# The feed-forward half as seven products of quarter matrices (Strassen's scheme), over three pairs of 366-column segments

## The chip, the cores and the metric

The kernel runs on one core of one Trainium2 chip. The metric is the device time of one execution in microseconds (us). Five engines of the core matter: PE (TensorE, the matmuls; its weight loads are listed as PEld), DVE (VectorE), ACT (ScalarE), POOL (GpSimd) and SP (SyncE, which here only issues DMAs). Each runs its own instructions in the order of the program; between engines, semaphores make an instruction wait for another's result. PE writes its sums to eight PSUM banks; everything else lives in SBUF, or in DRAM behind DMAs.

## The reference

One layer of a streaming encoder, on 2192 tokens (128 sample tokens of 8 streams, 16 meta tokens, 2048 prompt tokens) of 1024 channels. The first half is two mixers (an RWKV-7 and an mLSTM) with projections in and out, which the change doesn't touch. The second half is the feed-forward:

```
x  = x + concat(yA, yB) @ w_out
x  = x + (SiLU(dwconv3_causal(h2 @ W_act)) * (h2 @ W_gate)) @ w_down,  h2 = RMSNorm(x)
then one final RMSNorm.
```

W_act and W_gate are 1024 x 2816 each, w_down is 2816 x 1024, all float32. The convolution has three causal taps per channel.

## The kernel before, in words

Channels lie on the partitions (8 tiles of 128), tokens in the columns. The tokens are cut into six segments, one of 272 and five of 384 columns.

All large products are made of float32r matmuls: each operand is split into a high part (a cast on ACT) and a low part (the difference, on DVE), and each 128x128 weight tile against a segment takes three matmuls: high x high, high x low, low x high (`gemm`, L309 to L320).

The feed-forward (from L1131) goes over three groups of two segments. In each group 22 steps f make one tile of W_act and one of W_gate (`load_w`, L364: a DMA on SP's queue, the cast at L374, the difference through `tt` at L259), 24 matmuls of 8 input tiles each per segment; then the convolution and SiLU of the first (L1219 to L1239: PSUM is copied out to `ub`, one tap is a tensor_scalar at L1234, two are scalar_tensor_tensor at L1236, tanh on ACT at L1238, L1239), the product with the second at L1240 and the split of the result, gh on ACT (L1243) and gw on DVE and POOL in turns. After 4 or 5 such steps (CHUNKS) the down products of these f run: for each of 8 output tiles d and each segment 12 or 15 matmuls, and one DVE addition into the residual x (L1259). At the end of a group comes the final norm and the store (`rstd`, L1266, L1268). Weights are loaded and split again in each of the three groups.

The normed input h2 of the first two segments is made inside the first half (`ffn_acts`, L1055), in pools that both halves share, so the first feed-forward matmuls of the program's order stand among the last of the mixers. The output projection of the last segment (`last_out`, L1183) runs inside the feed-forward, in the first group's last chunk.

What sets the order: the kernel is written stage by stage, and the framework's scheduler orders the instructions of each engine from a simulated timeline and priorities (the table KN moves stages in it, `ranked`). PSUM's eight banks are rings by tag: gm 2, a 1, m 1, iv 2, ch 2.

Of the kernel before, what the change touches and what calls it, by code (L numbers as in the profile page):

```python
# [39 lines left out]

def staggered(segs, lag):
    """(tile, segment) pairs: each tile for all segments, a later segment lag tiles behind the one before."""
    return [(t - i * lag, g) for t in range(KD + lag * (len(segs) - 1)) for i, g in enumerate(segs) if 0 <= t - i * lag < KD]

# [12 lines left out]
def consts():  # L57
# [3 lines left out]
    c["ident"] = np.eye(128)  # L61
    c["id64"] = (s[:, None] == t[None]).astype(float)
# [15 lines left out]
    c["one"] = np.ones((128, 1))  # L78
# [14 lines left out]
# Places in the scheduler's order, engines, PSUM rings and buffer counts of the stages.  # L93
# [118 lines left out]
def trunk_kernel(ctx: ExitStack, tc: tile.TileContext, A):  # L212
# [50 lines left out]
    wp = ctx.enter_context(tc.tile_pool(name="wp", bufs=1))  # L263
    big = ctx.enter_context(tc.tile_pool(name="big", bufs=2))

    cst = cp.tile([128, CONST.shape[1]], F32, name="cst")
# [3 lines left out]
    def C(n, rows=128):  # L270
        o, w = COFF[n]
        return cst[:rows, o:o + w]
# [8 lines left out]
    ident, id64, blk, one = C("ident"), C("id64"), C("blk"), C("one")  # L281
# [55 lines left out]
    def token_sums(pr, acc, n):  # L337
        """Sums over the channels, tokens on the partitions."""
# [9 lines left out]
    def split_acts(name, half, n, src=None, scale=None, raws=None):  # L348
        """float32r parts of an activation tile: src is loaded, scale(raw, k, j) fills or scales tile k in raw[:, j]."""
# [14 lines left out]
    def load_w(src, cache=None):  # L364
        """float32r parts of a weight tile; parts that come again are kept in DRAM."""
# [21 lines left out]
    def pt(tag, shape=(128, 512)):  # L387
        """A bank, in the shape asked for."""
# [6 lines left out]
    with ExitStack() as p1:  # L395
        pool = lambda n, b, **k: p1.enter_context(tc.tile_pool(name=n, bufs=b, **k))
        kp = pool("kp", 1)
# [10 lines left out]
        nc.sync.dma_start(cst, A["cst"])  # L408
# [42 lines left out]
        def build_h0():  # L451
            """The first segment's activations: squares are summed over the channels by ones on the tensor engine."""
# [50 lines left out]
        def shifted(w, h, s, ct, out):  # L503
            """Projected columns of tile ct, each mixed with the token before it."""
# [115 lines left out]
        def rwkv(u, s, ws, h, lo1, lo2):  # L620
# [157 lines left out]
            def chain():  # L778
# [4 lines left out]
                def sb(t, h):  # L783
                    """S' and the rank-one updates' left factors of head h."""
# [101 lines left out]
        def conv4(w, h, s, j, out):  # L886
            """Projected columns, causal conv of four taps and SiLU; j is the channel tile of q|k."""
# [142 lines left out]
        def out_proj(s, ds):  # L1030
            """Residual plus the projected mixers' output, kept in DRAM."""
# [23 lines left out]
        def ffn_acts(s):  # L1055
            """The normed input of the second half, for the segments that come first there."""
            n = SEGS[s][1]
            rb = pt("gm")
            bcast(rb, rsd[:, s], n)
            return split_acts("h2", s, n, xd[s], lambda r, k: V.scalar_tensor_tensor(  # L1060
                r, r, PR("nf", k), rb[:, :n], op0=ALU.mult, op1=ALU.mult))

# [3 lines left out]
        H = {}  # L1066
# [12 lines left out]
        for s, u, hd in slots:  # L1079
# [36 lines left out]
            if s == len(SEGS) - 1 and u == 3:  # L1116
                with rank("h20"):
                    H[0] = ffn_acts(0)
            if u is None:
                with rank("h21"):  # L1120
                    H[1] = ffn_acts(1)
# [9 lines left out]
    with ExitStack() as p2:  # L1131
        pool = lambda n, b, **k: p2.enter_context(tc.tile_pool(name=n, bufs=b, **k))
        kp = pool("kp2", 1)
        accp = pool("acc", 4)
        gp = pool("gp", 1)
        ep = pool("ep2", 2)
        sp = pool("sp2", 2)
        rings = {x: itertools.cycle([t for t in y for _ in range(banks[t])]) for x, y in (("up", ("gm", "a")), ("dn", ("iv", "m")), ("rb", ("ch",)))}

        def pt2(use):  # L1140
            return pt(next(rings[use]), (128, NW))

        fst = kp.tile([128, NFF, 8, 2], F32, name="fst")
        nc.scalar.dma_start(fst, A["st_ffn"])
        h_f = kp.tile([128, NFF, 2], F32, name="h_f")
        so_ffn = kp.tile([128, NFF, 9, 2], F32, name="so_ffn")

        @ranked("sqs")
        def square_sum(acc, src, k, n):
            if k == 0:  # L1150
                S.activation(acc[:, :n], src, AF.Square)
                return
            q = ep.tile([128, NW], F32, name="nsq", tag="nsq")
            S.activation(q[:, :n], src, AF.Square)
            (V if k == KD - 1 else G).tensor_tensor(acc[:, :n], acc[:, :n], q[:, :n], op=ALU.add)

        @ranked("rstd")
        def rstd(acc, n):
            ss = token_sums(pt2("rb"), acc, n)
# [10 lines left out]
        def kparts(h, n):  # L1170
            return [(h[0][:, k, :n], h[1][:, k, :n]) for k in range(KD)]
# [181 lines left out]
```

## Time and profile before

| | |
|---|---|
| time, median of 3 runs | 3524.24 us (3522.81 to 3527.25) |
| profiled execution, span of its instructions | 3507.6 us |
| PE busy | 3411.7 us (97%) |
| DVE busy | 2146.4 us (61%) |
| ACT busy | 1152.2 us (33%) |
| POOL busy | 941.0 us (27%) |
| feed-forward, last mixer matmul to last matmul | 1877 to 3489 us |

The span is the time from the first to the last instruction of the one execution that the profiler took; the profile lists no other time of that execution. The median of the runs is 16.6 us above the span. Busy shares are means over two halves with different limits, so they are read by stretch below. A name such as ps_gm is a PSUM bank by its tag, w a split weight tile, h2hi and h2lo the split input.

### The profile page before, as it was taken

Reading aid. Unit: us, or ns where it says so; the run is one execution under the profiler, and the core shown is the slowest. Engines: PE = TensorE matmul, PEld = TensorE weight load, DVE = VectorE, ACT = ScalarE, POOL = GpSimd, SP = SyncE. Lnnn points to the kernel's source line nnn. Section 1 sums busy time; section 2 is a strip of 40 time slices with the busy share of each in tenths; the row PEclk is TensorE's granted clock in tenths of the full one; section 3 lists DMA queues with packets and bytes.
Section 4 is the critical chain, followed back from the end, with each engine's and each line's share of the span. In section 5 each row is a group of like instructions: output and inputs, shape, how many; then the busy total and the mean of one; then the engine's idle time right before and its main releaser. Section 6 shows DMA issues by size and latency. Waiting matters only on the chain.

```text
span 3507.6 us, 63114 instructions
## 1 busy us (share of the span) xinstructions
PE 3411.7 (97%) x24228; PEld 3123.6 (89%) x24228; DVE 2146.4 (61%) x5529; ACT 1152.2 (33%) x2826; POOL 941.0 (27%) x2294
## 2 busy tenths in 40 slices
PE   7999999999999999999989999999999999999998
PEld 6776888888888888888878999999999999999998
DVE  7777767666665776766665555574545447454544
ACT  5443444333433343343332222232222223222222
POOL 2532335434334444434421000021000012010002
PEclk9888999999999999999988999999999999999999
DMA  8753666455455545545523222232222233212221
GB/s 307 252 172 109 218 221 202 150 171 179 148 164 172 174 151 186 184 142 195 167 85 110 76 79 73 73 113 84 67 66 67 66 127 111 66 48 67 67 67 63
DMA packets 187565, 459.40 MB, mean 131 GB/s; under 512 B 68320, under 2 KB 111744, under 8 KB 156800
## 3 DMA queue, kind: packets, MB, share of 16 engines
q1 hardware_dynamic: 136648, 187.25, 18.0%
q0 software_dynamic: 28080, 204.48, 17.6%
q10 hardware_dynamic: 22536, 63.63, 4.8%
q8 instruction: 191, 3.13, 0.4%
q14 instruction: 110, 0.90, 0.1%
HBM read 381.68 MB, written 73.63 MB: 130 GB/s over the span
## 4 chain that ended last, share of the span: by engine, by line
PE 86%; DVE 6%; DMA 3%; ACT 2%; issue 1%; POOL 1%; ACTq 0%; SPq 0%; POOLq 0%; DVEq 0%
PE ps_gm L320 43%; PE ps_iv L320 11%; PE ps_a L320 10%; PE ps_m L320 5%; PE ps_iv L305 2%; PE ps_a L712 2%; PE ps_ch L826 1%; PE ps_ch L845 1%; PE ps_ch L839 1%; PE ps_iv L810 1%; PE ps_m L955 1%; DVE w L259 1%; DMA xt<-in_x_dram 1%; PE ps_a L305 1%; PE ps_m L972 1%
## 5 line engine op out<-in xcount | busy, mean ns | idle before, releaser
L320 PE MATMUL ps_gm<-hhi,w 128*128 128x384 f32 (+1 forms) x2976 | 813.1, 345 | 7.4 <-ACT w L374 2.2
L320 PE MATMUL ps_gm<-h2hi,w 128*128 128x384 f32 (+1 forms) x2816 | 701.1, 327 | 0.2 <-ACT ub L1221 0.2
L320 PEld LDWEIGHTS ps_gm<-hhi,w 128*128 128x128 f32 x2976 | 540.8, 193 | 30.2 <-issue 5.5
L320 PE MATMUL ps_gm<-hlo,w 128*128 128x384 f32 (+1 forms) x1488 | 502.2, 338 | 3.0 <-DVE hlo L360 3.0
L320 PEld LDWEIGHTS ps_gm<-h2hi,w 128*128 128x128 f32 x2816 | 500.0, 188 | 0.9 <-ACT ub L1221 0.5
L320 PE MATMUL ps_gm<-h2lo,w 128*128 128x384 f32 (+1 forms) x1408 | 459.9, 327 | 0.0
L374 ACT CAST w<-wraw 128x1024 fp32r<-128x1024 f32 (+2 forms) x291 | 259.4, 892 | 455.8 <-PE ps_iv L320 243.0
L320 PE MATMUL ps_iv<-gh,w 128*128 128x384 f32 (+1 forms) x1410 | 361.2, 330 | 0.0
L320 PE MATMUL ps_a<-h2hi,w 128*128 128x384 f32 (+1 forms) x1408 | 358.0, 327 | 0.0
L259 DVE TENSOR_TENSOR w<-wraw,w 128x1024 fp32r<-128x1024 f32 (+2 forms) x291 | 301.0, 1035 | 64.4 <-ACT w L374 60.4
L320 PEld LDWEIGHTS ps_gm<-hlo,w 128*128 128x128 f32 x1488 | 287.3, 193 | 9.5 <-DVE hlo L360 3.4
L320 PEld LDWEIGHTS ps_gm<-h2lo,w 128*128 128x128 f32 x1408 | 264.9, 188 | 0.0
L320 PEld LDWEIGHTS ps_iv<-gh,w 128*128 128x128 f32 x1410 | 252.5, 188 | 0.0
L320 PEld LDWEIGHTS ps_a<-h2hi,w 128*128 128x128 f32 x1408 | 251.0, 188 | 0.1
L320 PE MATMUL ps_iv<-gw,w 128*128 128x384 f32 (+1 forms) x705 | 232.6, 330 | 0.0
L320 PE MATMUL ps_a<-h2lo,w 128*128 128x384 f32 (+1 forms) x704 | 230.5, 327 | 0.0
L1238 ACT ACTIVATE fth<-ac 128x384 f32<-128x384 f32 (+1 forms) x132 | 67.2, 510 | 398.1 <-DVE ac L1236 388.7
L1231 POOL COPY h_f<-ub 128x2 f32<-128x2 f32 x88 | 16.4, 187 | 636.7 <-DVE ub L252 403.9
L320 PE MATMUL ps_m<-gh,w 128*128 128x384 f32 (+1 forms) x702 | 186.0, 330 | 0.0
L1259 DVE TENSOR_TENSOR x<-x,ps_iv 128x384 f32<-128x384 f32 (+1 forms) x160 | 85.3, 533 | 161.4 <-PE ps_iv L320 161.0
L1234 DVE TENSOR_SCALAR ac<-ub,d_fw,d_fb 128x384 f32<-128x384 f32 (+1 forms) x154 | 68.5, 457 | 182.8 <-ACT ub L248 157.1
L320 PE MATMUL ps_gm<-yhi,w 128*128 128x384 f32 (+1 forms) x640 | 168.3, 336 | 1.0 <-ACT yhi L359 0.7
(385 smaller groups left out, 6357.5 us busy)
## 6 DMA issues: line engine op xcount, KB each, us to landing
w<-wc POOLq DMA_DIRECT2D x155, 1024.0 KB, 5.4
wraw<-in_w_up_dram SPq DMA_DIRECT2D x132, 512.0 KB, 3.6
wc<-w ACTq DMA_DIRECT2D x31, 1024.0 KB, 6.5
wraw<-in_w_down_dram SPq DMA_DIRECT2D x72, 256.0 KB, 2.6
wraw<-in_w_in_dram SPq DMA_DIRECT2D x31, 512.0 KB, 5.9
wraw<-in_w_down_dram SPq DMA_DIRECT2D x48, 320.0 KB, 2.9
xraw<-in_xT_dram SPq DMA_DIRECT2D x36, 384.0 KB, 3.3
xt<-in_x_dram SPq DMA_DIRECT2D x15, 512.0 KB, 6.6
```

The lines of the kernel that those rows point to most:

```text
L259: (V if e[turn[name] % len(e)] == "V" else G).tensor_tensor(out, a, b, op=op)
L305: T.matmul(out[h:h + 64], lhsT[h:h + 64], rhs[h:h + 64], start=start, stop=stop)
L320: T.matmul(ps, w, x, start=i == 0, stop=i == len(seq) - 1)
L374: S.copy(hi[:, :nk], raw[:, :nk])
L712: T.matmul(psS[hs, i, X], kb[hs, X, cl(c)], ar[hs, h, :, cl(c)], start=True, stop=True)
L810: T.matmul(pp[hs, i], TA[hs, 0, i], sb(SC[c][hs].unsqueeze(1), h)[:, 0], start=True, stop=True)
L826: T.matmul(pd[hs, :64], ar[:, h, x, cl(c)], vz[:, h], start=True, stop=x == 0)
L839: T.matmul(pz[hs, :64], kb2[:, h], vz[:, h], start=True, stop=True)
L845: T.matmul(py[hs, :64], sc[hs, 64:128], vz[hs, h], start=False, stop=True)
L1234: V.tensor_scalar(av, view(2), fwh[:, 44 + f:45 + f], fbh[:, f:f + 1], op0=ALU.mult, op1=ALU.add)
L1238: S.activation(th[:, :n], ac[:, :n], AF.Tanh)
L1259: V.tensor_tensor(X[s][:, d, :n], X[s][:, d, :n], p, op=ALU.add)
```

## The change

The feed-forward goes over three pairs of equal segments (366, 366; 366, 366; 364, 364 columns) in place of the first half's unequal ones. Its matrices are taken as 2 x 2 blocks: a weight matrix A of blocks A11 to A22 and a matrix of activations B of blocks B11 to B22, and each block product A x B (4 block products) is made of 7 products of sums of blocks (the form of Strassen's scheme after Winograd). For the up products of one f the rows of A are the gate tile and the W_act tile, its columns the two halves of the 1024 channels; B is two halves of the channels by the two segments. For the down products A is a pair of output tiles by two halves of a chunk's f.

- Up: 7 products of 12 matmuls per f (84, before 96). Down: 7 products of 6 (chunks of 4 f) or 3 (the first chunk, 2 f) matmuls per pair of output tiles.
- The weight sums S1 to S4 are built in the first pair, on POOL and DVE; those of the up weights are kept in DRAM as they are (WU) and each of the 7 blocks is split again in every pair; those of the down weights are kept split (WD), and come back by DMA in the second and third pair.
- The sums of the input (`ffn_acts`) and of the gated result are built by `combine`, four operations on 366 columns per block position.
- A quad uses three PSUM banks. The first product is copied to SBUF by ACT (p1); the second and fourth, whose bank goes on being summed into, are added to p1 by DVE (P6, P67), and the rest is added on DVE, in down partly on POOL (p1, P6 and P67 into the residual).
- One tap of the convolution is now an Identity activation on ACT with scale and bias, and SiLU is one activation (before tanh, and an operation on DVE).
- `last_out` stands behind the first up steps of the first pair and writes its residual to DRAM.
- The second half's pools are its own; the first half's `wp` and `big` are given back when the mixers end, and h2 of the first two segments is made after that.

```diff
-GROUPS = [[0, 1], [2, 3], [4, 5]]
+PAIRS = [[(i * 732, NP), (i * 732 + NP, NP)] for i in range(2)] + [[(1464, 364), (1828, 364)]]
-CHUNKS = [(0, 5), (5, 10), (10, 14), (14, 18), (18, 22)]
+CHUNKS = [(0, 2), (2, 6), (6, 10), (10, 14), (14, 18), (18, 22)]
...
+        def split(dst, src, lo):
+            S.copy(dst[0], src)
+            lo.tensor_tensor(dst[1], src, f32(dst[0]), op=ALU.subtract)
...
+            eng[0].tensor_tensor(b11, b12, b11, op=ALU.subtract)
+            store("T1", b11)
+            eng[1].tensor_tensor(b12, b22, b12, op=ALU.subtract)
+            store("T3", b12)
...
+        def quad(Wb, Xb, n, after):
+            t1, t2, t3 = next(quads)
+            b1, b2, b3 = bank(t1)[:, :n], bank(t2)[:, :n], bank(t3)[:, :n]
+            product(b1, Wb("A11"), Xb["B11"], True, True)
+            after("P1", b1)
+            yield
+            product(b2, Wb("S2"), Xb["T2"], True, True)
+            after("P6", b2)
+            yield
+            product(b1, Wb("A12"), Xb["B21"], False, True)
+            after("C11", b1)
+            yield
+            product(b2, Wb("S3"), Xb["T3"], False, True)
+            after("P67", b2)
+            yield
+            product(b3, Wb("S1"), Xb["T1"], True, True)
+            after("P5", b3)
+            yield
+            product(b2, Wb("A22"), Xb["T4"], False, True)
+            after("C21", b2)
+            yield
+            product(b3, Wb("S4"), Xb["B22"], False, True)
+            after("C12", b3)
...
+            G.tensor_tensor(s1, a21, a22, op=ALU.add)
+            V.tensor_tensor(s2, s1, a11, op=ALU.subtract)
...
+            G.tensor_tensor(s3, a11, a21, op=ALU.subtract)
...
+            V.tensor_tensor(s2, a12, s2, op=ALU.subtract)
...
+                    t = wq.tile([128, 2, 4, 128], F32R, name="w2", tag="w2", bufs=4)
+                    split((t[:, 0], t[:, 1]), raw["t"][:, i % 2], V)
...
+                        nc.sync.dma_start(f32(t[:, :k]), f32(WD[key][:, i:i + k]))
...
+                    S.activation(av, view(2), AF.Identity, scale=PR("fw", 44 + f), bias=PR("fb", f))
+                    for i in (1, 0):
+                        V.scalar_tensor_tensor(av, view(i), PR("fw", i * 22 + f), av, op0=ALU.mult, op1=ALU.add)
+                S.activation(ac[:, :n], ac[:, :n], AF.Silu)
...
+                    V.tensor_tensor(held[what], b, held["p1"], op=ALU.add)
...
+                    if what == "P1":
+                        held["p1"] = wide("p1", "p1", 2)[:, :n]
+                        S.copy(held["p1"], b)
+                        add((1, 0), held["p1"], G)
+                    elif what in ("P6", "P67"):
+                        held[what] = wide(what, what, 2)[:, :n]
+                        V.tensor_tensor(held[what], b, held["p1"], op=ALU.add)
+                        add((0, 1) if what == "P6" else (1, 1), held[what], G)
+                    else:
+                        add({"C11": (0, 0), "P5": (1, 1), "C21": (1, 0), "C12": (0, 1)}[what], b, V)
...
+            for d in range(0, KD, 4):
+                steps(tiles(d), tiles(d + 2))
...
+                split(t, src, (V, G)[len(GB) % 2])
...
+                    for f in fs:
+                        up(p, f, H, graw)
+                        if due:
...
+                            down(p, X, *due)
...
+                    combine(graw[fs[0], 0], graw[fs[0], 1], graw[fs[1], 0], graw[fs[1], 1], store_g(GB), (V, V, V, V))
```

Two places of the program show what moved. The first is PE's order where the first half ends. Before, feed-forward matmuls (L320, from h2hi and h2lo) stand among the mixers' (L826, L305):

```order
L826 MATMUL ps_ch<-scs,ar 64x64 x2
L331 MATMUL ps_gm<-cst,rsd 128x128 x3
L305 MATMUL ps_iv<-TA,cL 64x64
L826 MATMUL ps_ch<-scs,ar 64x64 x2
L305 MATMUL ps_iv<-TA,cL 64x64 x3
L320 MATMUL ps_gm<-h2hi,w 128x272
L320 MATMUL ps_gm<-h2lo,w 128x272
```

In the changed kernel the mixers' last matmuls (mLSTM, L954 to L1018) all stand ahead of the first product of the feed-forward (L1206):

```order
L954 MATMUL ps_m<-rm,km 128x128
L955 MATMUL ps_m<-ngs,cst 128x128
L972 MATMUL ps_m<-vt,mw 128x129
L977 MATMUL ps_m<-cn_22775,rm 128x129
L996 MATMUL ps_m<-vt,kw 128x129
L1018 MATMUL ps_m<-cst,nd 128x128 x3
L1206 MATMUL ps_gm<-hb,w_23061 128x366 x12
L1206 MATMUL ps_iv<-hb,w_23078 128x366 x12
```

No feed-forward matmul is left among the mixers.

The second place is an up step, of the third group before and of the second pair after. On DVE before, a step of one segment is a copy out of PSUM, four operations of the convolution and SiLU, the product with the gate and every second gw; a 1024-column weight difference stands twice per f:

```order
L1234 TENSOR_SCALAR ac<-ub,d_fw,d_fb 128x384
L1236 SCALAR_TENSOR_TENSOR ac<-ub,d_fw,ac 128x384
L259 TENSOR_TENSOR w<-wraw,w 128x1024
L1236 SCALAR_TENSOR_TENSOR ac<-ub,d_fw,ac 128x384
L1239 SCALAR_TENSOR_TENSOR ac<-fth,ac 128x384
L1240 TENSOR_TENSOR ac<-ac,ps_gm 128x384
L259 TENSOR_TENSOR w<-wraw,w 128x1024
L252 COPY ub<-ps_a 128x384
```

After, 512-column weight differences (L1165) alternate with the sums of products (P6 and P67 at L1382, the W_act tile's second and first segment at L1386 and L1395):

```order
L1382 TENSOR_TENSOR P_33924<-ps_iv,p_33907 128x366
L1165 TENSOR_TENSOR w_33980<-wr,w_33980 128x512
L1165 TENSOR_TENSOR w_34013<-wr,w_34013 128x512
L1382 TENSOR_TENSOR P_33959<-ps_iv,p_33907 128x366
L1386 TENSOR_TENSOR ub<-ps_m,P_33959 128x366
L1165 TENSOR_TENSOR w_34071<-wr,w_34071 128x512
L1165 TENSOR_TENSOR w_34088<-wr,w_34088 128x512
L1395 TENSOR_TENSOR ub<-ps_iv,p_33907 128x366
L1165 TENSOR_TENSOR w_34108<-wr,w_34108 128x512
L1365 SCALAR_TENSOR_TENSOR ac<-ub,par,ac 128x366 x4
```

Two weight differences stand between P6 and P67 on DVE. On PE at the same step (the products of w_33964 and w_33944 are P5 and the second part of P67, that of w_33980 is C21, summed into P67's bank):

```order
L1206 MATMUL ps_iv<-hb,w_33909 128x366 x12
L1206 MATMUL ps_gm<-hb,w_33929 128x366 x12
L1206 MATMUL ps_m<-hb,w_33964 128x366 x11
L1206 MATMUL ps_iv<-hb,w_33944 128x366 x12
L1206 MATMUL ps_m<-hb,w_33964 128x366
L1206 MATMUL ps_iv<-hb,w_33980 128x366 x12
```

One matmul stands between the last of P67 and the first of C21, and DVE's addition P67 must have read the bank before C21 goes on in it.

## Rows read from the trace of the kernel before

**Rows 1.** The page's head: span, and each engine's busy time, share and instructions.

```profile
span 3507.6 us, 63114 instructions
PE 3411.7 (97%) x24228; PEld 3123.6 (89%) x24228; DVE 2146.4 (61%) x5529; ACT 1152.2 (33%) x2826; POOL 941.0 (27%) x2294
```

**Rows 2.** Windows: start:end, length, busy us (instructions) of each engine, granted clock, DMA, GB/s.

```profile
core 0: us, PE busy (x) PEld busy (x) DVE busy (x) ACT busy (x) POOL busy (x), PEclk, DMA share, GB/s
0.00:200.00 200.00, 169.79 (x1310) 140.64 (x1311) 151.70 (x508) 95.54 (x254) 69.59 (x197) 0.93 0.75 266
1700.00:1750.00 50.00, 49.32 (x430) 41.13 (x429) 34.19 (x107) 15.81 (x48) 28.06 (x71) 1.00 0.59 180
1750.00:1800.00 50.00, 41.06 (x349) 35.39 (x348) 34.62 (x94) 21.09 (x56) 18.34 (x45) 0.87 0.37 104
1804.00:1877.00 73.00, 62.97 (x473) 48.92 (x474) 42.72 (x152) 22.71 (x75) 12.12 (x24) 0.71 0.13 40
1877.00:3489.00 1612.00, 1612.00 (x9690) 1611.81 (x9690) 850.24 (x1465) 417.89 (x683) 195.55 (x408) 1.00 0.25 79
```

**Rows 3.** Lines, PE, 1877 to 3489 us: busy, mean ns, idle before and releaser.

```profile
L320 PE MATMUL ps_gm<-h2hi,w 128*128 128x384 f32 (+1 forms) x2784 | 694.5, 327 | 0.2 <-ACT ub L1221 0.2
```

**Rows 4.** Lines by form, DVE, 2400 to 2800 us.

```profile
L1236 DVE SCALAR_TENSOR_TENSOR ac<-ub,d_fw,ac 128x384 f32<-128x384 f32 x60 | 37.0, 617 | 3.4
L259 DVE TENSOR_TENSOR w<-wraw,w 128x1024 fp32r<-128x1024 f32 x30 | 36.7, 1223 | 7.8 <-ACT w L374 7.8
L1259 DVE TENSOR_TENSOR x<-x,ps_iv 128x384 f32<-128x384 f32 x42 | 23.3, 554 | 52.3 <-PE ps_iv L320 52.3
L259 DVE TENSOR_TENSOR w<-wraw,w 128x640 fp32r<-128x640 f32 x16 | 13.2, 824 | 1.8 <-ACT w L374 1.8
L259 DVE TENSOR_TENSOR w<-wraw,w 128x512 fp32r<-128x512 f32 x16 | 11.1, 693 | 1.0
L259 DVE TENSOR_TENSOR gw<-ac,gh 128x384 fp32r<-128x384 f32 x15 | 8.4, 557 | 8.7 <-ACT gh L1243 8.7
```

**Rows 5.** Lines by form, ACT, 2400 to 2800 us.

```profile
L374 ACT CAST w<-wraw 128x512 fp32r<-128x512 f32 x16 | 10.0, 622 | 34.4 <-PE ps_iv L320 24.8 <-PE ps_m L320 7.3 <-PE ps_gm L320 1.2
L1243 ACT CAST gh<-ac 128x384 fp32r<-128x384 f32 x30 | 15.4, 514 | 27.1 <-DVE ac L1240 26.0
```

**Rows 6.** Tiles gw and nacc, POOL: count, min/median/max ns, first and last start, forms.

```profile
L259 POOL TENSOR_TENSOR gw<-ac,gh x66: 1017/1379/1648, 1884.8 to 3456.8; 128x384 fp32r<-128x384 f32 x66
...
L1155 POOL TENSOR_TENSOR nacc<-nacc,nsq x42: 767/1018/2106, 2320.0 to 3488.4; 128x384 f32<-128x384 f32 x36, 128x272 f32<-128x272 f32 x6
```

**Rows 7.** Timeline, DVE and POOL in two up steps: start us, length us, instruction.

```profile
2369.41 1.14 POOL L259 TENSOR_TENSOR gw<-ac,gh 128x384 fp32r<-128x384 f32 x1
...
2369.78 1.84 DVE L1236 SCALAR_TENSOR_TENSOR ac<-ub,d_fw,ac 128x384 f32<-128x384 f32 x2
...
3444.18 1.27 DVE L1236 SCALAR_TENSOR_TENSOR ac<-ub,d_fw,ac 128x384 f32<-128x384 f32 x2
```

**Rows 8.** Where the halves meet: PE's waits (timeline), and tile h2hi from 1804 to 1877.

```profile
1794.18 0.45 PE L839 MATMUL ps_ch<-scs 128*64 128x64 f32 x2 [5.17 <-DVE scs L252]
...
1876.53 0.69 PE L320 MATMUL ps_gm<-h2hi,w 128*128 128x384 f32 x1 [0.17 <-ACT ub L1221]
...
L320 PE MATMUL ps_gm<-h2hi,w x33: 285/289/690, 1804.9 to 1876.5; 128*128 128x272 f32 x32, 128*128 128x384 f32 x1
```

**Rows 9.** Timeline, first half: PE waits for one DVE operation at a time.

```profile
1758.57 0.33 PE L305 MATMUL ps_iv<-wv,TA 64*64 64x64 f32 x4 [0.27 <-DVE wv L252]
...
1764.75 0.70 PE L305 MATMUL ps_iv<-wv,TA 64*64 64x64 f32 x8 [0.75 <-DVE wv L252]
```

**Rows 10.** Timeline of the end: last matmul of the products, last scaling.

```profile
3488.89 0.34 PE L320 MATMUL ps_iv<-gh,w 128*128 128x384 f32 x1
...
3499.82 4.29 DVE L1266 SCALAR_TENSOR_TENSOR x<-x,par,ps_ch 128x384 f32<-128x384 f32 x8 [2.96 <-PE ps_ch L331]
```

**Rows 11.** DMA issues: queue, count, KB each, median us to landing.

```profile
wraw<-in_w_up_dram SPq DMA_DIRECT2D x132, 512.0 KB, 3.6
...
xraw<-in_xT_dram SPq DMA_DIRECT2D x36, 384.0 KB, 3.3
```

More of the change, by code (lines that the diff above doesn't have):

```diff
@@ L1143, in trunk_kernel, with bank @@
-        fst = kp.tile([128, NFF, 8, 2], F32, name="fst")
-        nc.scalar.dma_start(fst, A["st_ffn"])
+        quads = itertools.cycle([("gm", "iv", "a"), ("gm", "iv", "m")])
+        last = len(SEGS) - 1
+        def bank(tag):
+            return pt(tag, (128, NW))
         h_f = kp.tile([128, NFF, 2], F32, name="h_f")
         so_ffn = kp.tile([128, NFF, 9, 2], F32, name="so_ffn")
[L1148 to L1155, printed above, removed]
@@ new lines, in norm_bank @@
+        def norm_bank(a, n):
+            rb = bank("ch")
+            for s, x0, x1, o0, o1 in pieces(a, n):
+                for i, (o, r) in enumerate(tok_tiles(SEGS[s][1])):
+                    lo, hi = max(x0, o), min(x1, o + r)
+                    if lo < hi:
+                        T.matmul(rb[:, o0 + lo - x0:o0 + hi - x0], rsd[:r, s, i:i + 1].to_broadcast([r, 128]), ident[:r, lo - o:hi - o], start=True, stop=True)
+            return rb
+        def split(dst, src, lo):
+            S.copy(dst[0], src)
+            lo.tensor_tensor(dst[1], src, f32(dst[0]), op=ALU.subtract)
@@ new lines, in product @@
+        def product(ps, w, x, start, stop):
+            for i, ((wh, wl), (xh, xl)) in enumerate(zip(w, x)):
+                for j, (l, r) in enumerate(((wh, xh), (wh, xl), (wl, xh))):
+                    T.matmul(ps, l, r, start=start and i + j == 0, stop=stop and i == len(x) - 1 and j == 2, skip_group_check=not start)
+        def quad(Wb, Xb, n, after):
[21 more added lines that the diff above has]
+            after("C12", b3)
@@ new lines, in down, with square_sum, tiles, add @@
+        def down(p, X, f0, f1, GB):
+            n = PAIRS[p][0][1]
+            Q = {}
+            def square_sum(j, d):
+                src = X[j][:, d, :n]
+                if d == 0:
+                    Q[j] = wide("ac", "ac", 2)[:, :n]
+                    S.activation(Q[j], src, AF.Square)
+                    return
+                q = wide("p1", "p1", 2)[:, :n]
+                S.activation(q, src, AF.Square)
+                G.tensor_tensor(Q[j], Q[j], q, op=ALU.add)
+            def tiles(d):
+                x = {(i, j): X[j][:, d + i, :n] for i in range(2) for j in range(2)}
+                held = {}
+                def add(at, what, eng):
+                    eng.tensor_tensor(x[at], x[at], what, op=ALU.add)
+                def after(what, b):
+                    if what == "P1":
+                        held["p1"] = wide("p1", "p1", 2)[:, :n]
+                        S.copy(held["p1"], b)
+                        add((1, 0), held["p1"], G)
+                    elif what in ("P6", "P67"):
+                        held[what] = wide(what, what, 2)[:, :n]
+                        V.tensor_tensor(held[what], b, held["p1"], op=ALU.add)
+                        add((0, 1) if what == "P6" else (1, 1), held[what], G)
+                    else:
+                        add({"C11": (0, 0), "P5": (1, 1), "C21": (1, 0), "C12": (0, 1)}[what], b, V)
+                return quad(down_weights(d, f0, f1), GB, n, after)
+            for d in range(0, KD, 4):
+                steps(tiles(d), tiles(d + 2))
+                if f1 == NFF:
+                    for e in range(d, d + 4):
+                        for j in range(2):
+                            square_sum(j, e)
+            return Q
```

373 lines of the change are left out of this document (245 added, 128 removed).

## The prediction

> **What bounds the kernel now.** The page's head comes first: PE is busy 97% of the span, DVE 61% [rows 1]. A mean over two unlike halves says little, so the windows come next. In the feed-forward PE is busy 1612.00 of 1612.00 us at a granted clock of 1.00, DVE 850 us, ACT 418, POOL 196 [rows 2]. PE's group by line waits 0.2 us in all that time [rows 3]. So this half lasts as long as its matmuls: 9690 of them in 1612 us, 0.1664 us each, at a mean of 365 columns, which is nearly the new width. The profiled execution's own time is not listed, only its span, 3507.6 us; the median of the runs stands 16.6 us above it, and I add that at the end.
>
> **Removed on PE.** The new order has 84 matmuls per f and pair (before 96), and in down 42 or 21 per pair of output tiles: 2772 per pair, 8316 in three pairs, against 9504, with 192 of the last output projection in both. 1188 x 0.1664 = 198 us less, if PE stays the bound. By pair PE needs 461 us; the first has 192 x 0.174 = 33 us more, 494.
>
> **What DVE gets.** Durations follow from rows of 384 or 512 columns. The weight differences of 1024, 640 and 512 columns took 1223, 824 and 693 ns [rows 4], a slope of 1.04 ns per column; by it an operation of 366 columns is 18 x 1.04 = 19 ns shorter than at 384: 0.598 us for a scalar_tensor_tensor, 0.538 for a tensor_tensor in SBUF, 0.535 from PSUM, and a 256-column difference 0.427, a 128-column one 0.294.
> - Up, per f in the second and third pair: 7 differences of 512 (4.85), 6 operations that read PSUM (3.21), 4 of the convolution (2.39), the gated product (0.54), 2 sums of the gated result (1.08), 0.8 low parts (0.44): 12.5 us, beside 84 x 0.1664 = 14.0 on PE. In the first pair 2 sums of weights and the sample tokens' pieces add 2.0: 14.5, above PE's 14.0.
> - Down, per pair of output tiles: 6 operations from PSUM, 3.2 us beside 42 x 0.1664 = 7.0 on PE. In the first pair 9 more of 256 columns: 7.05 (20 times), or 5.85 with 128 columns (4 times).
> - The next pair's input, 8 sums, 28 low parts and 16 scalings: 28 us; the final norm 8.6.
>
> Sums: first pair 22 x 14.5 + 20 x 7.05 + 4 x 5.85 + 28 + 9 + 8 (last projection) = 529 us; second 389; third 361. PE's are 494, 461 and 457. So DVE passes PE in the first pair and is near it in the others.
>
> **What POOL gets, and what that does to DVE.** POOL's additions of 384 columns took 1.017 us at best, of 272 columns 0.767 [rows 6]: 0.98 at 366, and by the same slope 1.30 at 512 and 0.73 at 256. The first pair has 252 of them (weight sums 92, residual 72, low parts 59, the rest 29), 247 us; the others some 150 each, 149 and 142 us. Before, 108 stood in the whole feed-forward. Here is the price: while POOL took 1.14 us for one from 2369.41, two DVE operations of two SBUF inputs took 1.84 us instead of 1.27 [rows 7], so DVE lost 0.57 us, half of POOL's time. POOL loses too: its median is 1379 ns, its longest 1648 [rows 6]. I take half of each POOL operation as DVE's loss; the ends are nothing (POOL runs beneath operations that read PSUM, or while DVE waits) and the whole. In the first pair that is 529 + 124 = 653 us, between 529 and 776. In the second and third DVE has 389 + 75 = 464 and 361 + 71 = 432, near PE's time, with ends of 538 and 503.
>
> The Trainium skill says of this pair of engines ("SBUF — State Buffer", section "Who interferes with whom") that a DVE instruction with two SBUF inputs contends with a GpSimd instruction that reads SBUF, and that whoever comes second is blocked until the first has finished. The row of 1.84 against 1.27 us agrees in kind; that the loss was half of POOL's time and not all of it can be the start of POOL's operation, which lay beneath DVE's one before. Read strictly, all such work of the two engines adds up; that is a rival below.
>
> **New waits of PE.** The second bank of a quad goes on being summed into: P6 and P67 must be read by DVE first. In the order one matmul (0.17 us) stands between P67's last and the next product in its bank, and weight differences of 0.69 us are queued on DVE ahead. The addition takes 0.535 us; a PE waiting for a single DVE operation stood 0.27 and 0.75 us [rows 9], and one difference in front adds up to 0.69. I take 1.2 us per f, 26 us per pair; the ends are nothing, and 3 us where DVE is late anyway, which is inside its own sum. What stands behind PE's waiting product in the queue is the next f's, so nothing fills the hole.
>
> **ACT.** 7 casts of 512 (0.62), about 3.5 of 366 (0.50), the copy, an Identity and a Silu for each segment, all near 0.5 [rows 5]: under 9 us per f, beneath DVE's 12.5. The Identity and Silu on ACT save DVE 2 x 2 operations per f; that is in its sum.
>
> **Where the halves meet.** Before, DVE's and ACT's work for the feed-forward lay in the mixers' tail, once with PE waiting 5.17 us behind it, and feed-forward matmuls filled PE's holes there, 33 of the high part in bank gm alone, 0.29 us each; the feed-forward goes on at 1876.53 without a break [rows 8]. Now the tail is the mixers' alone. It loses that wait and, as I estimate, 7 of those 10 us: I put its end at 1865, between 1848 (twice as much, and a second such wait) and 1877 (nothing). Then the input's work begins with PE idle: a load, 3.3 us [rows 11], 29 DVE operations of 0.55 before the first product (the first needs all four tiles of a block), 16 us, and 3.6 for casts and first weights: 23 us. The first product comes at 1888, between 1868 and 1912. PE's clock stood at 0.87 when PE was busy 82% of 1750 to 1800, and at 0.71 from 1804 [rows 2]; at 0.87 the first pair's matmuls would take 568 us, still below DVE's 653, so I add nothing for it.
>
> **DMA.** Cached splits of the down weights come at 1.84 MB per 7 us, 263 GB/s. The first 200 us ran at 266 GB/s with the DMA engines 75% busy [rows 2], so I cost it at nothing; a rival has the other end. Up brings 1.84 MB per 14 us, half the rate.
>
> **The sum.** First product 1888; first pair 653; second 461 + 26 + 10 (its input waits for the first pair's last products, 28 us of DVE beside 28 of PE and down's own 13) = 497; third 457 + 26 = 483; the end as before, 3507.6 - 3488.9 = 19, taken as 20 [rows 10]. 1888 + 653 + 497 + 483 + 20 = 3541 us, 33 above the span of before; with 16.6, **3557 us**. Of the 198 us that PE saves, the second and third pair keep about 95 against a third of 1612 each; the first pair gives back 116 against 537, and the junction 11.
>
> **Rivals.**
> 1. POOL hides: its operations fall beneath DVE's PSUM readers and waits. For it: a third of DVE's time in the first pair reads PSUM. Against: 1.84 against 1.27. First pair 529 + 24 (waits) = 553, the others 470 and 460: 1888 + 553 + 470 + 460 + 20 = 3391, time 3408. Chance 0.15.
> 2. The lock, well packed: in the first pair DVE's operations of two SBUF inputs (up 22 x 10.7 = 235, down 87, input 19, last projection 4: 345) and POOL's 247 add up to 592, everything else runs beside them. For it: DVE and POOL are queues of their own, and PSUM readers are between. 1888 + 592 + 470 + 460 + 20 = 3430, time 3447. Chance 0.20. This is what the page's rule gives.
> 3. The other side, and worse than my forecast: each POOL operation holds DVE for its whole length, in all three pairs, so that DVE bounds these too: 1888 + 776 + 538 + 503 + 20 = 3725, time 3742. It decides from about 0.75 of a POOL operation on (389 + 112 = 501, above the second pair's 497). For it: the 1648 ns of POOL's longest show both blocked. Against: the half above. Chance 0.12.
> 4. The down stage of pairs two and three waits for DMA: at 220 GB/s a quad takes 8.35 us instead of 7.0, 40 times: 54 us, time 3611. Against: 266 GB/s were reached. Chance 0.08.
>
> That the change doesn't do what it says is excluded by the count of matmuls in the order.
>
> **How the numbers follow.** Forecast 0.40, with its own range 3490 to 3630 (a quarter to three quarters of POOL's time, and the ends of the junction); rivals 0.15, 0.20, 0.12, 0.08; 0.05 left. A measurement of this kernel tells 0.2%, 7 us, from no change. Faster: rivals 1 and 2 and 0.08 of my own case, 0.43; the same 0.06; slower: 0.51. The range of 8 in 10 takes in rivals 2 and 4, half of rival 1 and stops short of rival 3: 3405 to 3700.
>
> **What would show it.** In the first pair DVE busy above 90% and PE with holes whose releaser is DVE's w2, P67 or ub; POOL's median on its additions above 1.2 us and DVE's 512-column differences above 0.75 us. In the second and third pair PE busy near 93%, waits of 1 to 1.5 us for P67 once per f. PE idle 15 to 30 us before the first product. It is wrong if DVE's differences keep 0.69 us beside POOL's work (rival 1), if PE is above 97% in the first pair, or if PE waits there for DMA.

## The result, and the profile after

The changed kernel takes 3683.64 us (median of 4 runs, 3674.44 to 3690.87), beside 3523.52 us before: a ratio of 1.0464, interval 1.0434 to 1.0494. Slower, as forecast, but by 160 us where 33 were forecast. It lies inside the range and beyond the likeliest case's own range, 3490 to 3630.

The page's head of the changed kernel, to be read against [rows 1]:

```profile
span 3676.8 us, 64591 instructions
PE 3354.0 (91%) x23050; PEld 2987.4 (81%) x23050; DVE 2587.7 (70%) x6399; ACT 1435.6 (39%) x3557; POOL 1406.1 (38%) x2675
```

PE has 1178 matmul records fewer (of 1188 matmuls less), but only 58 us less busy time, and stands without work for 323 us of the span instead of 96. The windows, with the columns of [rows 2]: the three pairs (cut at each pair's first up matmul), then an up and a down stage of the first pair, its first and last down stage, and a down and an up stage of the second pair:

```profile
core 0: us, PE busy (x) PEld busy (x) DVE busy (x) ACT busy (x) POOL busy (x), PEclk, DMA share, GB/s
1896.50:2585.60 689.10, 577.64 (x2987) 531.57 (x2987) 536.04 (x1013) 281.27 (x606) 294.58 (x340) 0.91 0.50 171
2585.60:3131.40 545.80, 493.85 (x2804) 476.01 (x2805) 395.04 (x686) 215.44 (x414) 182.52 (x225) 0.97 0.52 168
3131.40:3651.10 519.70, 482.02 (x2804) 466.30 (x2802) 357.28 (x624) 200.18 (x380) 168.62 (x217) 0.99 0.50 165
2145.00:2201.00 56.00, 53.36 (x313) 52.46 (x314) 52.90 (x96) 29.53 (x58) 21.47 (x25) 1.00 0.43 147
2099.50:2143.50 44.00, 33.54 (x156) 28.77 (x156) 30.25 (x62) 13.29 (x34) 20.84 (x25) 0.88 0.53 196
1990.00:2038.00 48.00, 32.51 (x123) 26.77 (x122) 23.25 (x65) 11.06 (x36) 20.16 (x28) 0.73 0.69 219
2513.00:2586.00 73.00, 44.29 (x162) 33.86 (x161) 59.19 (x107) 29.69 (x72) 39.95 (x40) 0.74 0.42 142
2725.00:2756.00 31.00, 28.98 (x170) 28.06 (x169) 16.79 (x32) 5.38 (x12) 12.00 (x14) 1.00 0.64 204
2849.50:2907.50 58.00, 55.23 (x324) 54.09 (x324) 44.51 (x74) 29.11 (x55) 14.46 (x21) 1.00 0.42 140
```

In the first pair's up stage DVE is busy 94% and PE 95%. In its down stage neither is the bound: DVE 69%, PE 76%, at a granted clock of 0.88, while the same stage of the second pair takes 31 us at 1.00. PE's matmuls also took longer than at the full clock: at the 0.1705 us of busy time per matmul of that full-clock stage (28.98/170) the three pairs' matmuls would keep PE busy 509, 478 and 478 us; they took 578, 494 and 482, 88 us more. By the trace's clock records PE was busy for 125 us of the three pairs at the lower of its two levels, half speed, so about 62 of the 88 us are the clock's. The rest goes with the holes themselves: at full clock each unbroken run of PE is listed some 0.26 us longer than its matmuls at 0.1675 us each, and the three pairs have 211 such runs. In the feed-forward of before the clock was 1.00 [rows 2].

What waits in the down stage of the first pair, 2099.5 to 2143.5: engine, tile and line, whom it waited for, us in total, times, longest.

```profile
ACT w L1164 <- DMA wd<-w: 14.1, 8, 4.3
...
DVE w L1165 <- ACT w L1164: 7.4, 7, 1.6
POOL ws L1254 <- DVE w L1165: 5.6, 5, 2.1
...
ACT w L1164 <- POOL ws L1254: 4.8, 4, 1.3
...
ACT w L1164 <- DVE ws L1248: 4.2, 2, 2.5
...
PE ps_m L1206 <- DVE w L1165: 4.0, 2, 3.6
...
PE ps_a L1206 <- ACT w L1164: 2.8, 2, 2.2
```

It is a chain: POOL sums two blocks, DVE sums on, ACT casts, DVE takes the difference, PE multiplies, and ACT may not begin the next cast into a tile while that tile's last content is on its way to DRAM. Each engine waits for another; none is full.

Where the halves meet and at the end, to be read against [rows 8] and [rows 10]:

```profile
1869.36 0.90 PE L1018 MATMUL ps_m<-cst,nd 128*128 128x128 f32 x3 [2.46 <-DVE nd L1016]
1896.49 3.76 PE L1206 MATMUL ps_gm<-hb,w 128*128 128x366 f32 x12 [26.23 <-ACT w L1164]
```

```profile
3651.36 6.42 POOL L1417 TENSOR_TENSOR ac<-ac,p 128x364 f32<-128x364 f32 x7 [3.74 <-ACT p L1416]
...
3656.91 1.38 PE L338 MATMUL ps_ch<-cst,ac 128*128 128x1 f32 x6 [5.81 <-POOL ac L1417]
```

PE stood 26.23 us before the first product, and at the end for a chain of seven square sums on POOL.

### The profile page after: what moved, and what is told of

Same layout as the page of the kernel before. It is cut to its first block, busy times and chain, and to the rows that moved or that the text cites. A ratio compares the mean times of both kernels' runs of the same rounds, so it can differ in the third digit from the quotient of the medians.

```text
span 3676.8 us, 64591 instructions
## 1 busy us (share of the span) xinstructions
PE 3354.0 (91%) x23050; PEld 2987.4 (81%) x23050; DVE 2587.7 (70%) x6399; ACT 1435.6 (39%) x3557; POOL 1406.1 (38%) x2675
## 5 line engine op out<-in xcount | busy, mean ns | idle before, releaser
L1206 PE MATMUL ps_iv<-hb,w 128*128 128x366 f32 (+1 forms) x2376 | 440.0, 333 | 27.5 <-ACT g L1164 12.7
L1206 PEld LDWEIGHTS ps_iv<-hb,w 128*128 128x128 f32 x2376 | 405.4, 191 | 35.2 <-ACT g L1164 15.8
L1165 DVE TENSOR_TENSOR w<-wr,w 128x512 fp32r<-128x512 f32 (+2 forms) x446 | 318.7, 719 | 95.5 <-ACT w L1164 87.0
L1164 ACT CAST w<-wr 128x512 fp32r<-128x512 f32 (+2 forms) x446 | 258.1, 582 | 327.5 <-PE ps_iv L1206 190.4
L1206 PE MATMUL ps_gm<-hb,w 128*128 128x366 f32 (+1 forms) x1584 | 305.9, 338 | 54.1 <-ACT w L1164 31.9
L1206 PEld LDWEIGHTS ps_gm<-hb,w 128*128 128x128 f32 x1584 | 273.0, 193 | 67.4 <-issue 26.5
L1165 POOL TENSOR_TENSOR g<-gr,g 128x366 fp32r<-128x366 f32 (+1 forms) x177 | 204.9, 1170 | 258.1 <-ACT g L1164 257.6
L1206 PE MATMUL ps_iv<-g,w 128*128 128x366 f32 (+1 forms) x1188 | 258.1, 356 | 26.4 <-DVE P L1433 8.6
L1206 PEld LDWEIGHTS ps_iv<-g,w 128*128 128x128 f32 x1188 | 217.8, 205 | 44.8 <-ACT w L1164 16.8
L1206 PE MATMUL ps_gm<-g,w 128*128 128x366 f32 (+1 forms) x792 | 171.7, 352 | 40.4 <-DMA w<-wd 23.7
L1206 PEld LDWEIGHTS ps_gm<-g,w 128*128 128x128 f32 x792 | 141.9, 201 | 54.3 <-DMA w<-wd 24.9
L1365 DVE SCALAR_TENSOR_TENSOR ac<-ub,par,ac 128x366 f32<-128x366 f32 (+3 forms) x308 | 174.7, 610 | 12.7 <-ACT ac L1363 9.3
```

What stands on the lines that cost most here:

```text
L1164: S.copy(dst[0], src)
L1165: lo.tensor_tensor(dst[1], src, f32(dst[0]), op=ALU.subtract)
L1206: T.matmul(ps, l, r, start=start and i + j == 0, stop=stop and i == len(x) - 1 and j == 2, skip_group_check=not start)
L1365: V.scalar_tensor_tensor(av, view(i), PR("fw", i * 22 + f), av, op0=ALU.mult, op1=ALU.add)
```

## The experiments

Times are told as the ratio to the kernel before, run on the same chip, and its 95% interval. "First" is the start of the first product; the pairs are cut as above, in the one profiled run. All in us but the ratio. A pair that an edit hardly touches still differs by up to 9 us from kernel to kernel (the third with e5, 511 against 520), so single differences of that size say little.

| kernel | ratio (interval) | first | pairs | span |
|---|---|---|---|---|
| changed | 1.0464 (1.0434 to 1.0494) | 1896 | 689, 546, 520 | 3677 |
| e1_no_store | 1.0393 (1.0358 to 1.0428) | 1897 | 674, 540, 514 | 3652 |
| e2_pool_no_reads | 1.0137 (1.0109 to 1.0165) | 1895 | 634, 529, 502 | 3569 |
| e3_one_input | 1.0330 (1.0307 to 1.0354) | 1891 | 670, 520, 522 | 3629 |
| e4_x_on_sp | 1.0424 (1.0401 to 1.0447) | 1881 | 698, 542, 511 | 3659 |
| e5_ready_down | 1.0144 (1.0120 to 1.0167) | 1893 | 608, 540, 511 | 3577 |
| e6_long_fills | 1.0199 (1.0177 to 1.0221) | 1898 | 663, 528, 502 | 3602 |
| e7_ready_quiet | 0.9893 (0.9867 to 0.9919) | 1898 | 561, 521, 498 | 3487 |
| e8_all_four | 0.9770 (0.9737 to 0.9802) | 1895 | 554, 499, 493 | 3450 |
| e9_built_early | 1.0504 (1.0480 to 1.0527) | 2009 | 611, 535, 513 | 3693 |
| e10_built_spread | 1.0478 (1.0450 to 1.0506) | 2003 | 610, 541, 512 | 3691 |

**No store of the split weights.**

```diff
-                        nc.scalar.dma_start(f32(WD[key][:, i + 1 - k:i + 1]), f32(t[:, :k]))
...
```

> The split down weights are not stored in the first pair; the second and third pair load as many bytes, in the same pieces, from another tensor in DRAM, so their down products use other weights. Theory A (the first pair's down stage is held up because a weight tile stays taken until its store to DRAM has landed, and ACT's next cast waits for that): the first pair falls from 689 us to about 600, its down stages from 0.28 us per matmul to 0.20, the waits of ACT for these stores are gone, time about 3595 us. Theory B (the prediction's: DVE, slowed by POOL, is the bound of the first pair): DVE's work and POOL's stay the same, so the first pair stays near 690 us and the time near 3684.

The ratio fell by 0.007 (25 us), the first pair by 15 us, to 674, where theory A had some 600 and theory B some 690. The same down stage, and ACT's longest waits in it:

```profile
2091.40:2130.10 38.70, 30.56 (x149) 26.84 (x148) 32.02 (x60) 13.54 (x34) 20.87 (x24) 0.91 0.17 55
```

```profile
ACT w L1164 <- PE ps_iv L1206: 7.5, 7, 1.5
ACT w L1164 <- POOL ws L1254: 6.4, 4, 1.9
ACT w L1164 <- DVE ws L1248: 4.4, 2, 2.7
```

The waits for the stores are gone, and others took their place. Theory A named one link of the chain, and not the chain.

**POOL's operations read nothing.**

```diff
-            lo.tensor_tensor(dst[1], src, f32(dst[0]), op=ALU.subtract)
+            if lo is G:
+                G.memset(f32(dst[1]), 0.0)
+                return
+            lo.tensor_tensor(dst[1], src, f32(dst[0]), op=ALU.subtract)
...
-            G.tensor_tensor(s1, a21, a22, op=ALU.add)
+            G.memset(s1, 0.0)
...
```

> In the second half every addition and difference of POOL is replaced by a fill of its output with a constant, which reads nothing: its sums of weights, low parts, residual additions and square sums are left out. Theory B (POOL's reads slow DVE, and DVE is the bound): the 87 us by which DVE's operations in the first pair are longer than their shortest vanish, and the 41 and 31 us in the others too; the time falls by 125 to 160 us, to 3525 to 3560. Theory A (the stores' buffers are the bound of the down stage): only the first pair's up stages, where DVE is busy 94%, gain, some 20 us, and a little in the others; time 3640 to 3665, the first pair's down stage still above 0.26 us per matmul.

115 us less (ratio 1.0464 to 1.0137), a little less than theory B's 125 to 160; but only 55 of it in the first pair, 17 in each of the others and 17 at the end, where the square sums' chain is a fill too. The first pair's down stages stayed at 0.25 to 0.28 us per matmul, near theory A's figure. A fill of 366 columns takes 0.40 us, the additions took 0.9 to 1.2, so this run can't part POOL's reads from POOL's lateness; the next does in part.

**Fills as long as the additions.**

```diff
+        def slow(t, v):
+            G.memset(t, v)
+            G.memset(t, v)
+            G.memset(t[..., :t.shape[-1] // 2], v)
...
```

> As the kernel in which POOL's additions in the second half were fills that read nothing, but each fill made to last as long as the addition did: two whole and one half fill, 0.40 + 0.40 + 0.24 us. What POOL computes is left out again. Theory B (POOL's reads hold up DVE's operations of two SBUF inputs): DVE's operations stay short, excess over their shortest near 13 us in the whole half and not 164, and the time stays near that kernel's 3565, at most 3585. Rival F (it was POOL's lateness: its results, the weight sums, the low parts and the residual, came sooner): the time goes back most of the way, to 3640 to 3680, with DVE's operations short all the same.

93 us of the 115 stay gone, of which 15 are the end; the time, 3599 us, lies between theory B's 3585 and rival F's 3640. DVE by form (line, names and shapes, count | busy us, mean ns | idle before) from 1900 to 2580 us, first in the changed kernel:

```profile
L1165 DVE TENSOR_TENSOR w<-wr,w 128x512 fp32r<-128x512 f32 x65 | 59.6, 917 | 10.7 <-ACT w L1164 10.6
...
L1165 DVE TENSOR_TENSOR w<-ws,w 128x256 fp32r<-128x256 f32 x80 | 42.0, 530 | 36.3 <-ACT w L1164 36.3
...
L1365 DVE SCALAR_TENSOR_TENSOR ac<-ub,par,ac 128x366 f32<-128x366 f32 x44 | 39.4, 896 | 1.1 <-ACT ac L1363 0.4
```

and with the long fills:

```profile
L1173 DVE TENSOR_TENSOR w<-wr,w 128x512 fp32r<-128x512 f32 x73 | 49.9, 688 | 11.0 <-ACT w L1169 9.9
...
L1173 DVE TENSOR_TENSOR w<-ws,w 128x256 fp32r<-128x256 f32 x80 | 33.6, 420 | 32.1 <-ACT w L1169 32.1
...
L1373 DVE SCALAR_TENSOR_TENSOR ac<-ub,par,ac 128x366 f32<-128x366 f32 x44 | 26.2, 596 | 0.2
```

917 against 688 ns, 530 against 420, 896 against 596, with POOL nearly as busy as before (276 us of the first pair, 295 in the changed kernel): it is the reading that lengthens DVE. Added up over all groups of DVE in the second half, what lies above a group's 5th percentile fell from 164 us (91, 42 and 31 by pair) to 12 (13 with short fills). The three pairs with the long fills, to be read for DVE's own work:

```profile
1897.80:2560.50 662.70, 576.14 (x3005) 536.13 (x3006) 460.50 (x1021) 282.21 (x610) 276.08 (x835) 0.90 0.52 177
2560.50:3088.90 528.40, 486.35 (x2806) 472.47 (x2805) 361.72 (x684) 213.48 (x411) 170.26 (x531) 0.98 0.54 174
3088.90:3590.90 502.00, 475.01 (x2805) 464.53 (x2806) 334.98 (x628) 199.06 (x380) 161.28 (x508) 0.99 0.52 171
```

The Trainium skill ("SBUF — State Buffer", section "Who interferes with whom") says that such DVE operations contend with a GpSimd instruction that reads SBUF, and not with one that only writes it; this pair of kernels agrees on both halves of it. The changed kernel's trace shows the size of a single loss too. A weight difference that takes 0.68 us alone began while POOL's addition had 0.78 us left, and took 0.65 us longer:

```profile
2792.04 0.98 POOL L1165 TENSOR_TENSOR g<-gr,g 128x366 fp32r<-128x366 f32 x1 [4.46 <-ACT g L1164]
2792.24 1.33 DVE L1165 TENSOR_TENSOR w<-wr,w 128x512 fp32r<-128x512 f32 x1
```

In 192 of 234 such meetings in the second half (an operation of DVE with two SBUF inputs begins at least 0.05 us after one of POOL, with at least 0.2 us of it left) the loss is what was left of POOL's operation less 0.13 us (within 0.04): DVE waits it out. So the price of a POOL operation is not a fixed share of its length; it depends on when DVE's operation comes.

In the first pair, though, at most 26 us go by the reads: the other 29 of the 55 come back with the length of POOL's operations, rival F, which sits in the chain. The 26 are not the reads' alone: a fill also waits for no source and holds none, and how much that gives was not tried. At the end it is what counts, since 15 us are gone there with fills of full length. In the first pair's down stages nothing was gained, they took 0.27 to 0.30 us per matmul; the up stages went from 0.183 to 0.174.

**Down weights ready made.**

```diff
-                parts = a_parts(h[0][0], h[0][1], h[1][0], h[1][1], new)
-                WD[key] = dr.tile([128, 8, 2, kh, 128], F32R, name=f"wd{d}_{f0}")
+                WD[key] = cached = True
...
```

> The first pair too loads its down weights ready made, as the others do (all three pairs from another tensor in DRAM, so with other weights): the sums of the down weights on POOL and DVE, their splits on ACT and DVE, and the stores are left out. Theory E (what makes the first pair's down stages long is the building of the weights on the way, chain and all, of which the stores are only a part): the down stages of the first pair come to the 0.185 to 0.19 us per matmul of the later pairs, the first to 0.25, the last to 0.33; 61 + 24 + 14 = 99 us less, 689 to 590 us in the first pair, time about 3585. Rival (they wait for POOL's residual additions and low parts, which stay): above 0.24 us per matmul, time above 3630.

113 us less by the ratios, 81 in the first pair; its down stages are those of the later pairs. One of them:

```profile
2177.60:2207.20 29.60, 28.04 (x165) 27.13 (x164) 15.96 (x32) 4.41 (x9) 11.71 (x13) 1.00 0.62 202
```

29.6 us at a clock of 1.00, against 44.0 at 0.88. Theory E holds, and the rival (POOL's residual additions, which are still there) falls. The pair gave 18 us less than expected since its up stages became longer, 0.191 us per matmul and not 0.183 over the pair: DVE is nearly full there (54.59 of 63 us, in the row below). Probably work that had been done ahead in the slow down stages now falls into them; that was not tried.

```profile
2210.00:2273.00 63.00, 58.26 (x328) 56.70 (x327) 54.59 (x99) 30.22 (x59) 32.04 (x34) 0.95 0.46 154
```

**One input for all pairs.**

```diff
-                H = ffn_acts(p + 1)
+                H = {k: [(hi[:, :m], lo[:, :m]) for hi, lo in v] for k, v in H.items()}
```

> The second and third pair reuse the first pair's input: its loads, scalings, sums and splits for them are left out (32 scalings, 16 sums and 56 splits). Theory C (at a pair's end the next pair's input on DVE and ACT delays the last down products and the first up products): the last down stages of the first two pairs (0.42 and 0.33 us per matmul) come near 0.28 and 0.20, the first up stages of the second and third pair (0.25 and 0.21) near 0.19; 25 + 18 + 15 + 7 us less, time about 3620. Rival (what delays the pairs' joints is the load of the residual behind the final store): 15 us at most, time about 3670.

47 us less, where theory C had 65 and the rival 15: 19 and 26 in the pairs whose end carried the next input (and 6 at the start, which I can't explain). The third pair, from which theory C took 7 us, kept its length. Theory C holds for most of the joints, but not all: the last down stage of the first pair still took 53.3 us, at a clock of 0.81.

**The residual's loads on SP's queue.**

```diff
-                                    load_x(t, a, n, 0, KD, nc.scalar)
+                                    load_x(t, a, n, 0, KD, nc.sync)
```

> The loads of the residual for a pair go through SP's queue and not ACT's. Theory D (at a pair's start ACT stands behind these loads, 7.1 and 6.4 us in the second pair, because they wait for the final store of the pair before): these waits of ACT go, 10 to 25 us less in time, about 3665. Rival: SP's weight loads now stand behind the same wait, and the time stays within 10 us of 3684.

In the changed kernel ACT's copy stood 7.09 us behind these issues, which wait for the final store:

```profile
2610.47 0.54 ACTq L1147 DMA_DIRECT2D x<-xd  x1
2611.05 0.47 ACT L1379 COPY p<-ps_gm 128x366 f32<-128x366 f32 x1 [7.09 <-DMA out_o_y_dram<-x]
```

The ratios differ by 0.004 with intervals that overlap: 14 us, unclear in total. The second and third pair became 4 and 8 us shorter, the first product came 15 us sooner, and the first pair took 9 us more. The pairs' joints are not mainly these loads.

**The causes together.** Two kernels with the edits above combined.

> Both: the down weights come ready made in all pairs, and POOL's additions are fills (0.4 us). If the two causes add up in the first pair, as theories B and E have it, that pair comes to 689 - 99 - 55 + 10 (POOL's weight sums are in both) = 545 us and the time to 3684 - 99 - 119 + 10 = 3476. If they are two names for one (DVE's and POOL's work on the down weights), the first pair stays above 575 and the time above 3505.

> All four edits: down weights ready made, POOL's additions fills, one input for all pairs, the residual's loads on SP's queue. If the four account for what the pairs take beyond their matmuls (494, 461, 461 us), what is left is the first chunk of each pair and about 0.7 us of waits per f: 530, 485 and 480 us; time 3476 - 50 - 20 = about 3400, below the kernel before. If a further cause is left, the second and third pair stay above 500 us.

The two causes add up, nearly: the first pair came to 561 us, 128 us less, where the two edits alone gave 81 and 55. The ratio is 0.9893, 1.1% below the kernel before, from two runs; span 3487 where 3476 was given as the time. With all four it is 0.9770, also from two runs, and pairs of 554, 499 and 493, where I had 530, 485 and 480. The pairs of this last kernel:

```profile
1895.00:2449.00 554.00, 518.73 (x2988) 509.35 (x2989) 374.97 (x768) 213.65 (x414) 114.92 (x293) 0.97 0.58 190
2449.00:2948.00 499.00, 480.59 (x2798) 469.18 (x2797) 336.01 (x625) 201.45 (x381) 77.96 (x217) 0.99 0.53 175
2948.00:3441.00 493.00, 473.99 (x2803) 463.10 (x2802) 335.10 (x625) 199.99 (x380) 77.96 (x214) 1.00 0.53 174
```

So even with the building of the down weights, two thirds of the input's work and POOL's additions left out, 198 us of matmuls less come to 81 us by the ratio.

**Could the building be done elsewhere?** Two kernels build the down weights in the mixers' half, two quads behind a step (e9) or mostly one (e10). Both also load the residual through SP's queue and give half of the last pair's square sums to DVE, and all three pairs load the weights.

```diff
+            if 1 <= s <= 3:
+                for _ in range(2):
+                    build_down(*build.pop(0))
...
```

> A version that computes all: the down weights' sums and splits are made in the first half (two of the 24 quads behind each of the 12 steps of its second to fourth segment, in the rings of the projection weights) and stored; all three pairs load them. The residual's loads go through SP's queue, and in the last pair half of the square sums' additions through DVE. Theory E: the feed-forward's first pair is that of the kernel with ready-made weights, 608 us; 108 + 20 + 4 us less, if the first half hides the work as far as DVE (busy 76% there) has room: 92 us of DVE, 67 of ACT, 47 of POOL and the rings of projection weights; I take 30 us of it as seen, time 3684 - 132 + 30 = about 3580, still above the kernel before. Rival: the first half has no room, its PE waits for projection weights behind the stores, and it grows by 90 us or more: 3640 and above.

> The same, with the 24 quads spread over the second to sixth segment, one behind most steps. Theory E with a price for crowding: less is seen in the first half than with two behind a step, time 3565 to 3580. Rival: the quads in the last segment lengthen the tail of the mixers, where PE has holes, and the first product of the feed-forward comes later: 3585 to 3610.

Neither helped; their intervals overlap the changed kernel's, and the rival of e9 (90 us or more) came. The first pair is 611 and 610 us, as with ready-made weights, but the first product comes at 2009 and 2003 us, 112 and 107 us later. The same 800 us of the mixers' half, of the changed kernel and then of e9:

```profile
400.00:1200.00 800.00, 779.66 (x6363) 663.96 (x6363) 536.52 (x1619) 309.17 (x895) 341.93 (x837) 0.98 0.55 180
```

```profile
400.00:1200.00 800.00, 737.35 (x5791) 624.77 (x5789) 558.36 (x1643) 320.56 (x937) 332.57 (x793) 0.93 0.61 210
```

DVE has room there by its busy share, 67%, and PE still loses 9% of its matmuls in the window: a free engine is not a free path. I had 30 us for it. Which wait lost the time there was not tried. No version was found that does the whole layer and beats the kernel before.

## Why the prediction was wrong, by its steps

| step | forecast | measured |
|---|---|---|
| first product | 1888 | 1896 |
| first pair | 653 | 689 |
| second pair | 497 | 546 |
| third pair | 483 | 520 |
| end | 20 | 26 |
| span | 3541 | 3677 |

- **The step that failed: each pair as the load of its fullest engine.** The first pair was put at DVE's own work plus half of POOL's, the later ones at PE's matmuls plus two small waits, and whatever the other engines do was taken to hide behind that. The span missed by 136 us: 8 before the first product, 36, 49 and 37 in the pairs, 6 at the end.
- **In the first pair DVE is not the bound.** It is busy 536 of 689 us. Only the up stages run near DVE's limit (94% in the one shown). The down stages, which I costed by DVE's 7.05 us, ran by the chain of sums, casts, differences and stores, at 69% of DVE: e5 shows 81 us in the pair for the building, and e1 gives the stores 15. That 653 came within 36 us of 689 is luck: two terms too high stood where the chain was missing.
- **In the later pairs PE is the fullest engine, and the rest doesn't hide.** In the second pair the 49 us are 33 of PE's busy time (17 at the price of full clock, 0.1705 us a matmul in place of 0.1664, with 38 small ones of the norms that I had left out; 16 for holes and clock) and 16 of waiting (52 in place of 36). In the third the 37 are 25 and 12. e8, with all four edits, brings these pairs to 499 and 493 us, near the 497 and 483 that I had.
- **The number of matmuls: right.** 1178 records fewer.
- **DVE's own work: too high, and its agreement with the measured busy time is luck.** DVE was busy 536, 395 and 357 us, where I had 529, 389 and 361 without POOL's part; but the measured times have POOL's part in them. With the long fills, which leave DVE all its operations, it is 460, 362 and 335.
- **The price of POOL's reads: mechanism right, size wrong.** POOL's reads lengthen DVE's operations, and e6 shows it. The loss was some 164 us in the whole half, a quarter of the 646 us that POOL was busy and not half of 247 + 149 + 142. The row of 1.84 against 1.27 us was one meeting, and said nothing of how often they meet. Its effect on the time was at most 26 us in the first pair where 124 were put, and at most 18 in each of the others where nothing was put, since there I took DVE to be hidden.
- **"At 0.87 ... I add nothing for it": wrong.** That would hold if DVE were the bound. In a chain PE's slower matmuls lengthen each turn; PE's busy time is 88 us above the full-clock figure, 68 of it in the first pair.
- **The joints, put at 10 us: too small.** e3 gives 19 and 26 us to the next pair's input alone, beside the residual's loads behind the final store.
- **DMA at nothing: too small.** In the later pairs PE waits for the cached weights, rival 4's mechanism; the tile wd, and who waited for it (us, times):

```profile
  PE ps_gm L1206: 23.7, 26
...
  PE ps_m L1206: 6.3, 9
```

About 30 us over two pairs, where the rival had 54. The down stage there takes some 0.186 us per matmul, not 0.166, so that 42 matmuls cost 7.8 us, and 48 at the old price 8.0: the saving in down is nearly gone even where nothing else goes wrong.
- **P67's wait, 1.2 us per f: wrong.** In both later pairs together PE waited for such an addition (L1382) 3 times, 2.4 us in all, where 52 us were put. From 2849.5 to 2907.5, nearly four f's, PE has waits of 2.8 us, and takes 1.0 us per f above the matmuls' forecast price; the releasers are ACT's cast of g, of w and DVE's difference.
- **Where the halves meet: right.** 26.23 us of waiting, 23 forecast; the mixers ended at 1870 and not 1865.
- **Rivals 1 and 2 (faster)** gave 3408 and 3447. Even e7, without the building of the down weights and without POOL's reads, took 3489. Rival 3 gave 3742, nearer to the time than the forecast, by a mechanism that the runs refute: DVE was never busy for 776 us.

What stays open: how the 88 us of longer matmuls part into cause and consequence was not tried by itself, since each edit that fills PE's holes raises the clock too; whether more buffers in the rings of the weights would have loosened the chain; and of the joints, what remains after e3 and e4.

## What to carry to other kernels

A stage of several engines in a row, each waiting for the one before, takes its turn-around time and not the busy time of its fullest engine: add up one turn (sum, cast, difference, product, store landing, over the buffers that are free) before costing a new step by an engine's load. An engine that is the fullest does not hide the others either: here the later pairs had PE at 90% and 93% and still took 86 us more than forecast. A kernel whose PE is full at a clock of 1.00 has much to lose from holes, since here its matmuls slowed down with them. And a saving of an eighth of the matmuls must be set against every operand that has to be made for it: here the steady stages alone kept 6% in up and 2% in down.

## What the runs showed of the hardware that was not expected

- POOL's fills of the same length as its additions left DVE's operations near their shortest (excess 12 us of the half, against 164): for the length of DVE's operations only the reads count.
- PE's granted clock fell to 0.73 and 0.74, a mixture of its two levels (1.2 and 2.4 GHz), in stretches in which PE was busy 68% and 61% (1990 to 2038, 2513 to 2586); busy time per matmul there was 0.264 and 0.273 us, against 0.1705 at 1.00, with the holes' share in it.
- Building 24 sets of weights in the mixers' half cost 107 to 112 us, more than DVE's 92 us of work in it.
